# Hybrid attention and gMLP block in fp32: where tiles 3 and 4 of x are put, and when late weights and constants are loaded

## The chip, the cores and the metric

One core of a Trainium2 chip runs the whole block as one program. The metric is the time on the device in microseconds (us); lower is better. Three runs of the kernel before took 920.85, 924.07 and 924.38 us, so the median is 924.07 us. The profile comes from one further execution.

## The reference, cut to what matters

Everything is float32, with 1024 tokens and 1024 channels. One RMSNorm feeds one wide input projection. Two branches are computed from it, gated, summed, projected and added to x, and a last RMSNorm follows.

```python
h = rmsnorm(x, norm_g[l])
proj = h @ w_in[l]
q, k, v, za, u, vs, zs, gm = jnp.split(proj, IN_SPLITS, axis=-1)
...
a = window_sink_attention(q, k, v, att_sinks[l])
a = (a * jax.nn.silu(za)) @ w_att_out[l]
sgo = chunked_spatial_gating(jax.nn.gelu(u, approximate=False),
                             jax.nn.gelu(vs, approximate=False),
                             sg_w[l], sg_b[l], sg_ln_g[l], sg_ln_b[l])
sgo = (sgo * jax.nn.silu(zs)) @ w_sg_out[l]
ga, gs = jnp.split(jax.nn.sigmoid(gm + b_merge[l]), N_BRANCHES, axis=-1)
x = x + (ga * a + gs * sgo) @ w_o[l]
...
return rmsnorm(x, final_g)
```

The change lies in the first tenth of the program: the normalisation of x, the projection that makes `vs`, and the loads of what follows (the LayerNorm over `vs`, the mixing matrices and the projection that makes `u`).

## The kernel before, in words

**Products.** Each fp32 operand is split into a high and a low part in the type fp32r (`split`: ScalarE casts the high part, VectorE subtracts it to get the low one), and a product is three matmuls: high by high, high by low, low by high. On top of that every 1024-wide product is a two by two block scheme with seven block products instead of eight (Winograd's form of Strassen). For tokens the seven forms of the activations are called b11, t1, t2, b21, t3, b22, t4; each has a high and a low buffer of 128 x 4 x 512 (`T_b11h`, `T_t1l` and so on, one buffer each, made by `slot`). The weights' forms are a11, a12, s1, s2, s4, s3, a22.

**The first stage, `vs` (L703 to L862).** x comes in as eight tiles of 128 tokens. `scale_of(t)` loads a tile (unless it is in `x_in` already), squares it on ScalarE (L545) and makes the reciprocal root on VectorE; `turned_half` scales half of it in place on VectorE (L553) and transposes it on TensorE (L557) into a PSUM bank with the tag "sc", of which there are two. Tiles 0 to 3 (`first_tile`) give b11 and b21; tiles 4 to 7 (`second_tile`) give t1 and b22, and on the way a plain copy for t2, t3 and t4. Two DMAs with an add finish the latter for each of these tiles (`add_on`, L601 and L605, issued by GpSimd).

**Weights of `vs`.** a11 and a12 are loaded straight (into the places T_t3h and T_t3l). s1 is loaded into T_t4h in two halves, and then three pairs of adding DMAs run one behind the other, issued by GpSimd (L722 to L727): s1 += a22, a11 += s1 (this makes s2), a12 += a11 (this makes s4). s4 is split into `wh`, `wl` by `split_w("s4", c, behind=True)` (L746). s3 is loaded later into T_t4h again (L756) and added to (L758); a22 comes into two `wr` buffers (L764).

**Order of the matmuls.** `first_product(0..3)` (b11 by a11, b21 by a12), `by_s1(0)`, `by_s1(1)`, `by_s4(0)`, `by_s4(1)`, `by_s1(2)`, `by_s1(3)`, `by_s4(2)`, `by_s4(3)`, then three `late_product`s (t2 by s2, t3 by s3, t4 by a22). `by_s1` and `by_s4` are 12 matmuls of 128x512 for each tile. `gemm_pair` then makes `u`: its first call needs the first job's weights `r0` and `r1` and four sums of them (`make_sums`, L241 to L245, VectorE), which are split in turn by `split_next`.

**Queues.** Plain loads are all issued by SyncE (SP), adding DMAs by GpSimd (POOL); each engine issues in order, and a load waits at the head of its queue until its place is free. `raw_tile()` is a ring of three buffers with the tag "wr": x, a22 and the later weights go through it in turn. `after` orders two instructions of one engine; `behind` and `paced` make a DMA wait for a matmul, so that it is not sent too early. The order of the instructions on each engine is made by a scheduler from these constraints.

What follows is issued in this order by SP before the change: x0, a11, x1, a12, x2, the broadcast of norm_g (L716), s1, x3, x4, the first bias row (L889), x5, x6, x7, then behind the last transpose s3, a22 (L764), the mixing matrices (L789) and `r0`; behind the t2 product the five small constants (L831 to L841); then `r1`, whose `wr` buffer is the one of the first half of a22.

Of the kernel before, what the change touches and what calls it, by code (L numbers as in the profile page):

```python
# [24 lines left out]
F32 = mybir.dt.float32  # L25
# [5 lines left out]
P = 128  # L31
D = 1024
S = 1024
KC = D // P
# [18 lines left out]
def hybrid_tile(  # L53
# [16 lines left out]
    nc = tc.nc  # L70
# [15 lines left out]
    def mtile(shape, dt, tag, bufs, pool=None):  # L86
        return (pool or main).tile(shape, dt, name=nm(tag), tag=tag, bufs=bufs)
# [4 lines left out]
    def raw_tile():  # L92
        return mtile([P, D], F32, "wr", 3)
# [16 lines left out]
    sink_sb = const.tile([P, 8], F32, name="sink_sb")  # L110
    nsink_sb = const.tile([P, 8], F32, name="nsink_sb")
    bm_sb = const.tile([P, 16], F32, name="bm_sb")
    lg_sb = const.tile([P, KC], F32, name="lg_sb")
    lb_sb = const.tile([P, KC], F32, name="lb_sb")
# [43 lines left out]
    def after(second, first):  # L158

        tc.add_manual_dep(  # L160
            second.ins,
            first.ins.name,
            mybir.DependencyInfo(mybir.DependencyClass.NoSync, mybir.DependencyReason.DATA),
            reason="order",
        )
# [5 lines left out]
    def slot(name, shape=(P, 4, HALF), dt=F32R):  # L171

        return mtile(list(shape), dt, "T_" + name, 1)
# [28 lines left out]
    def begin_job():  # L202
        n = len(begun)
        if n < written[0]:
            begun.append(n)
            units.extend(jobs[n]())
# [25 lines left out]
    def half_of(half):  # L232
        return slice(half * HALF, (half + 1) * HALF)
# [46 lines left out]
    def paced(move):  # L280

        if pace[0] is not None:
            tc.add_manual_dep(
                move.ins,
                pace[0].ins.name,
                mybir.DependencyInfo(mybir.DependencyClass.Sync, mybir.DependencyReason.DATA),
                reason="pace",
            )
# [42 lines left out]
    term_of_x11 = [None]  # L331
# [149 lines left out]
    pool = outer.enter_context(tc.tile_pool(name="mixing", bufs=1))  # L481
# [4 lines left out]
    def load_x(t):  # L486
        xt = raw_tile()
        nc.sync.dma_start(xt[:], x[t * P : (t + 1) * P, :])
        return xt

    x_in = {0: load_x(0)}
# [18 lines left out]
    nf12 = [xtile() for _ in range(4)]  # L510
    f22 = []
# [4 lines left out]
    def x_place(i, j, t):  # L516
        return xh[:, 4 * j + t % 4, half_of(i)]
# [11 lines left out]
    casts, lows, turns = [], [], []  # L529

    def add_on(dst, src):
        return nc.gpsimd.dma_start(dst, src, accum_op=ALU.add)

    def behind(move, first):
        tc.add_manual_dep(
            move.ins,
            first.ins.name,
            mybir.DependencyInfo(mybir.DependencyClass.Sync, mybir.DependencyReason.DATA),
            reason="pace",
        )  # L540
# [48 lines left out]
    def second_tile(t):  # L589
        xt, r = scale_of(t)  # L590
        if t == 4:
            hb.update(new_b(("t1", "b22")))
            f22.append(slot("t4l", dt=F32))
        pt = turned_half(xt, r, 0)
        nc.vector.tensor_sub(raw_sum(t), raw_sum(t), pt[:])
        nc.scalar.mul(nf12[t - 4][:], pt[:], -1.0)
        form_of("t1", t, by_k(raw_sum(t)))
        pt = turned_half(xt, r, 1)
        form_of("b22", t, by_k(pt[:]))
        nc.scalar.copy(f22[0][:, t - 4, :], pt[:])  # L600
        add_on(nf12[t - 4][:], f22[0][:, t - 4, :])  # L601

    def raw_t2(t):
        nc.vector.tensor_add(raw_sum(t), raw_sum(t), f22[0][:, t - 4, :])
        return add_on(raw_b21(t), raw_sum(t))  # L605

    def w_vs(i, j, c):
        return w[W_VS + 4 * i + 2 * j + c]

    def two_k(v, c):  # L610
        return v[:, 2 * c : 2 * c + 2, :]

    def flat(v):
        return v.rearrange("p k n -> p (k n)")

    raws = {}

    def load_part(name, at, i, j, late=False):
        raws[name] = slot(at, dt=F32)
        for c in range(2):  # L620
            move = nc.sync.dma_start(flat(two_k(raws[name], c)), w_vs(i, j, c))
            if late:
                behind(move, turns[-1])

    def load_vs(c):
        nc.sync.dma_start(flat(two_k(raws["a11" if c < 2 else "a12"], c % 2)), w[W_VS + c])
# [34 lines left out]
    def vs_product(acc, name, t, weight, fresh, last=True, cs=(0, 1)):  # L661
        bh, bl = hb[name]
        for c in cs:
            for n in range(3):
                for k in (2 * c, 2 * c + 1):
                    wh, wl = vs_w[weight, k]
                    lt = (bh, bh, bl)[n][:, k, tokens(t)]
                    rt = (wh, wl, wh)[n]
                    mm = nc.tensor.matmul(
                        acc[:],  # L670
                        lt,
                        rt,
                        start=fresh and k == 0 and n == 0,
                        stop=k == 3 and n == 2,
                        skip_group_check=True,
                    )
        return mm

    accs = {}
    t5s = {}  # L680
# [10 lines left out]

    def by_s1(t):
        t5s[t] = bank("o" if t < 2 else "sc")
        vs_product(t5s[t], "t1", t, "s1", True)
        nc.scalar.mul(x_place(1, 1, t), t5s[t][:], -1.0)

    def by_s4(t):
        vs_product(t5s[t], "b22", t, "s4", False)
# [13 lines left out]
    for c in (2, 3):  # L712
        load_vs(c)
    x_in[2] = load_x(2)
    g_sb = xh[:, 6:8, HALF:D]
    nc.sync.dma_start(g_sb, norm_g.partition_broadcast(P).rearrange("p (h n) -> p h n", h=2))  # L716
    load_part("s1", "t4h", 1, 0)
    for c in (2, 3):
        split_vs(c)
    for move in unsplit:  # L720
# [23 lines left out]
    first_product(3)  # L744
    for c in range(2):
        split_w("s4", c, behind=True)  # L746
    second_tile(6)
    raw_t2(4)
    by_s1(0)
    by_s1(1)  # L750
    second_tile(7)
    for t in range(4):
        to_x11(t)
    for t in (5, 6, 7):
        last_of_h = raw_t2(t)
    load_part("s3", "t4h", 1, 0, True)  # L756
    for c in range(2):
        after(add_on(flat(two_k(raws["s3"], c)), w_vs(0, 0, c)), last_of_h)  # L758
    by_s4(0)
    by_s4(1)  # L760
    a22 = []
    for c in range(2):
        a22.append(raw_tile())
        behind(nc.sync.dma_start(a22[c][:], w_vs(1, 1, c)), turns[-1])  # L764
    by_s1(2)
    by_s1(3)
    split_w("s2", 0, behind=True)
# [13 lines left out]
    def gelu_of(t, half=0):  # L781
        two = xh[:, t : t + 2, half_of(half)]
        after(nc.scalar.activation(two, two, AF.Gelu), last_cast)
        if half == 0:
            for i in range(2):
                after(statistics(t + i, 0), lows[-1])

    mix_w = mtile([P, KC, P], F32, "wT", 1, pool)
    behind(nc.sync.dma_start(mix_w[:], sg_w), turns[-1])  # L789
    ones = mtile([P, P], F32R, "ones", 1, pool)  # L790
    nc.vector.tensor_scalar(ones[:], ident[:], 0.0, 1.0, op0=ALU.mult, op1=ALU.add)

    def late_product(name, weight, done, aside):
        for c in range(2):
            for t in range(4):
                pace[0] = vs_product(accs[t], name, t, weight, False, cs=(c,))
                if t % 2:
                    part_of_early(1)
                if c:
                    done(t)  # L800
                if aside:
                    aside.pop(0)()
# [25 lines left out]
        + [lambda: gelu_of(0), lambda: gelu_of(2)],  # L828
    )
    row_sums = [bank("sc") for half in range(2)]  # L830
    paced(nc.sync.dma_start(lg_sb[:], ln_g))  # L831
    paced(nc.sync.dma_start(lb_sb[:], ln_b))
    paced(nc.sync.dma_start(bm_sb[:], b_merge))
    of_head = sinks.rearrange("(c e r) -> e c r", e=2, r=2)
    for e in range(2):
        paced(
            nc.sync.dma_start(
                sink_sb[e * 64 : (e + 1) * 64].rearrange("p (c r) -> p c r", r=2),
                of_head[e].partition_broadcast(64),
            )  # L840
        )  # L841
    split_w("s3", 1)
    after(nc.vector.memset(mix_w[64:128, :, 0:64], 0.0), lows[-1])
    wh, wl = pair_of_w()
# [12 lines left out]
    split_w("a22", 1, a22[1][:])  # L857
    part_of_early(1)
    begin_job()
    late_product("t4", "a22", to_x21, [split_next, lambda: gelu_of(4, 1), lambda: gelu_of(6, 1)])  # L860
    for _ in range(2):
        split_next()  # L862
# [4 lines left out]
    late = []  # L867
# [17 lines left out]
    def bias_of(half):  # L885

        wT = mix_w[:, half * 4 : half * 4 + 4, :]
        bg = mtile([P, 4, P], F32, "bias", 1, pool)
        nc.sync.dma_start(bg[:].rearrange("p g i -> p (g i)"), sg_b[half_of(half)].partition_broadcast(P))  # L889
        for gg in range(4):  # L890
            g = half * 4 + gg
            nc.vector.scalar_tensor_tensor(
                bg[:, gg, :], row_sums[half][:, gg * P : (gg + 1) * P], lb_sb[:, g : g + 1], bg[:, gg, :], op0=ALU.mult, op1=ALU.add
            )
        return bg, wT

    bias = []
# [46 lines left out]
    pool = stage.enter_context(tc.tile_pool(name="keys", bufs=1))  # L944
# [44 lines left out]
    pool = stage.enter_context(tc.tile_pool(name="queries", bufs=1))  # L989
# [199 lines left out]
    pool = stage.enter_context(tc.tile_pool(name="attention", bufs=1))  # L1189
# [187 lines left out]
    pool = stage.enter_context(tc.tile_pool(name="later", bufs=1))  # L1377
# [508 lines left out]
```

## Time and profile before

| what | value |
|---|---|
| median of three runs | 924.07 us |
| profiled execution, its own time | 924.99 us |
| its span, first to last instruction | 923.2 us |
| mean granted clock of TensorE | 0.993 |
| TensorE busy with matmuls | 898.0 us |
| VectorE busy | 697.0 us |
| ScalarE busy | 527.3 us |
| GpSimd busy | 141.4 us |
| DMA moved | 209.57 MB, 227 GB/s in the mean |

A row of the timeline has the start in us, the busy time in us, the engine, the source line, the operation, the tile written and the tiles read, the shape, how many such instructions were merged, and in brackets how long the engine was idle before and what released it. A row of the windows has the busy time of each engine (and its number of instructions), the granted clock of TensorE, the DMA engines' busy share and the rate. A row of the chain of waits has start, duration and what the end of the program hung on in that time. "PE" is TensorE, "DVE" VectorE, "ACT" ScalarE, "POOL" GpSimd, "SPq" the queue of SyncE.

### The profile page before, as it was taken

The numbers are of one execution on the slowest core, as the hardware profiler recorded it, in microseconds if no ns is written. First come the engines' busy times: TensorE is split into PE (matmuls) and PEld (weight loads), VectorE is DVE, ScalarE is ACT, GpSimd is POOL, SyncE is SP. The second block draws the span as 40 slices with busy tenths as digits, with TensorE's granted clock in tenths as the row PEclk, the third lists the DMA queues.
The fourth block names the chain that finished last, engine by engine and source line by source line (L and its number), as shares of the span: only waits on it lengthen the run. The fifth ranks groups of instructions, "written<-read, shape, count | busy, mean of one in ns | idle before, by whom it ended". The sixth has DMA issues, their size and how long they took to land.

```text
span 923.2 us, 13181 instructions
## 1 busy us (share of the span) xinstructions
PE 898.0 (97%) x4284; PEld 746.0 (81%) x4284; DVE 697.0 (75%) x1263; ACT 527.3 (57%) x1058; POOL 141.4 (15%) x204
## 2 busy tenths in 40 slices
PE   8899899999999999999999999999998999999996
PEld 5678688888888778888888888888877887888885
DVE  6767786665678678887778888747797589579986
ACT  7666433334445366767766766755675475467443
POOL 1222112213011001111111111101100111210012
PEclk9999999999999999999999999999999999999999
DMA  8978878876788677778787788899869664998632
GB/s 292 220 179 213 248 237 179 175 151 200 245 282 259 228 222 182 186 184 200 196 207 235 251 245 188 225 318 369 307 212 324 243 197 153 308 299 287 205 114 115
DMA packets 131598, 209.57 MB, mean 227 GB/s; under 512 B 12649, under 2 KB 61033, under 8 KB 131530
## 3 DMA queue, kind: packets, MB, share of 16 engines
q1 hardware_dynamic: 110072, 149.74, 49.5%
q0 software_dynamic: 21312, 58.73, 27.9%
q8 instruction: 34, 0.56, 0.3%
q14 instruction: 34, 0.28, 0.1%
q10 hardware_dynamic: 146, 0.27, 0.1%
HBM read 147.74 MB, written 86.11 MB: 253 GB/s over the span
## 4 chain that ended last, share of the span: by engine, by line
PE 75%; DVE 10%; DMA 9%; issue 2%; ACT 1%; SPq 1%; POOL 0%; DVEq 0%; ACTq 0%; POOLq 0%
PE ps_mm L342 35%; PE ps_o L342 25%; PE ps_sc L1216 3%; DMA T_t4h<-in_w_dram 3%; PE ps_tp L342 3%; PE ps_o L1301 2%; PE ps_sc L342 2%; DMA wr<-in_w_dram 2%; PE ps_tp L1260 2%; DVE wl L156 2%; PE ps_tp L903 1%; DMA T_t3h<-T_t4h 1%; DVE bq L185 1%; DMA T_t3l<-T_t3h 1%; DVE bn L779 1%
## 5 line engine op out<-in xcount | busy, mean ns | idle before, releaser
L155 ACT CAST wh<-s 128x1024 fp32r<-128x1024 f32 (+1 forms) x78 | 78.2, 1005 | 95.6 <-PE ps_mm L342 49.4
L156 DVE TENSOR_TENSOR wl<-wr,wh 128x1024 fp32r<-128x1024 f32 (+1 forms) x78 | 73.1, 939 | 51.4 <-ACT wh L155 50.8
L155 ACT CAST wh<-wr 128x1024 fp32r<-128x1024 f32 (+1 forms) x78 | 64.0, 823 | 61.5 <-PE ps_mm L342 33.6
L156 DVE TENSOR_TENSOR wl<-s,wh 128x1024 fp32r<-128x1024 f32 (+1 forms) x78 | 91.0, 1166 | 10.5 <-ACT wh L155 10.3
L342 PE MATMUL ps_o<-T_t1h,wh 128*128 128x512 f32 x148 | 58.9, 398 | 0.7 <-ACT wh L155 0.7
L342 PE MATMUL ps_mm<-T_b11h,wh 128*128 128x512 f32 x140 | 55.8, 398 | 3.8 <-ACT xh L811 3.8
L342 PE MATMUL ps_mm<-T_b11h,wl 128*128 128x512 f32 x140 | 55.9, 399 | 2.9 <-DVE wl L156 2.9
L342 PE MATMUL ps_o<-T_b22h,wh 128*128 128x512 f32 x148 | 58.2, 393 | 0.0
L342 PE MATMUL ps_o<-T_b22l,wh 128*128 128x512 f32 x148 | 57.9, 391 | 0.0
L342 PE MATMUL ps_o<-T_b22h,wl 128*128 128x512 f32 x148 | 57.8, 390 | 0.0
L342 PE MATMUL ps_o<-T_t1h,wl 128*128 128x512 f32 x148 | 57.7, 390 | 0.0
L342 PE MATMUL ps_o<-T_t1l,wh 128*128 128x512 f32 x148 | 57.6, 389 | 0.0
L342 PE MATMUL ps_mm<-T_t4h,wh 128*128 128x512 f32 x140 | 55.6, 397 | 0.8 <-DVE x L377 0.8
L342 PE MATMUL ps_mm<-T_b11l,wh 128*128 128x512 f32 x140 | 55.8, 398 | 0.0
L342 PE MATMUL ps_mm<-T_t3l,wh 128*128 128x512 f32 x140 | 54.6, 390 | 0.6 <-DVE T_t3l L156 0.6
L342 PE MATMUL ps_mm<-T_t4h,wl 128*128 128x512 f32 x140 | 55.0, 393 | 0.0
L342 PE MATMUL ps_mm<-T_t3h,wh 128*128 128x512 f32 x140 | 54.9, 392 | 0.0
L342 PE MATMUL ps_mm<-T_t4l,wh 128*128 128x512 f32 x140 | 54.8, 391 | 0.0
L342 PE MATMUL ps_mm<-T_t3h,wl 128*128 128x512 f32 x140 | 54.7, 391 | 0.0
L1229 ACT ACTIVATE pr<-ps_sc,sm 128x192 f32<-128x192 f32 (+2 forms) x128 | 50.9, 410 | 6.6 <-DVE sm L1225 5.5
L342 PE MATMUL ps_mm<-T_t2l,wh 128*128 128x512 f32 x140 | 54.6, 390 | 0.0
L342 PE MATMUL ps_mm<-T_t2h,wl 128*128 128x512 f32 x140 | 54.6, 390 | 0.0
(384 smaller groups left out, 2399.8 us busy)
## 6 DMA issues: line engine op xcount, KB each, us to landing
wr<-in_w_dram SPq DMA_DIRECT2D x86, 256.0 KB
sums<-in_w_dram POOLq DMA_DIRECT2D x20, 512.0 KB, 9.3
s<-sums SPq DMA_DIRECT2D x20, 512.0 KB
q_hl<-qhl SPq DMA_DIRECT2D x16, 512.0 KB
q<-q_hl SPq DMA_DIRECT2D x64, 128.0 KB
y_dr<-x POOLq DMA_DIRECT2D x28, 256.0 KB, 6.5
wr<-in_w_dram SPq DMA_DIRECT2D x12, 512.0 KB
g<-in_w_dram POOLq DMA_DIRECT2D x12, 512.0 KB, 6.4
```

The source lines that it names most:

```text
L155: nc.scalar.copy(hi, src)
L156: return nc.vector.tensor_sub(lo, src, hi.bitcast(F32))
L185: op(dst[:, i : i + 2, :], a[:, i : i + 2, :], c[:, i : i + 2, :])
L342: nc.tensor.matmul(acc, lt, rt, start=fresh and k == 0 and n == 0, stop=k == 3 and n == 2, skip_group_check=True,)
L779: return nc.vector.bn_stats(stats[:, t, half, :], xh[:, t, half_of(half)])
L903: nc.tensor.matmul(pm[:, t * P : (t + 1) * P], xh[:, half * 4 + t, g * P : (g + 1) * P], bias[-1][1][:, g % 4, :], start=True, stop=True,)
L1216: nc.tensor.matmul(sc[:, i, k0:], q_of[:, c, i * P : (i + 1) * P], kt[:, f, k0:], start=f == 0, stop=f == 1,)
L1229: nc.scalar.activation(held_in[c, i], sc[:, i, lo:hi], AF.Exp, bias=nmax[:, c, i : i + 1], scale=-1.0, accum_out=sums[:, c, i : i + 1],)
L1260: nc.tensor.transpose(dst, pr[:, i, block * P : block * P + width], ident[:])
L1301: nc.tensor.matmul(po[:, cs], lt, rt, start=n == 0, stop=n == len(terms) - 1)
```

## The change

Tile t of x for t = 3 and 4 goes into T_t1l, the place of the low part of t1, which is not filled before tile 4 has been read. All of x is loaded from one place, and the first load of s1 stands ahead of the broadcast of norm_g. s3, a22, the small constants, the mixing matrices and the first bias row are issued behind the last matmul of `by_s1(0)` or `by_s1(1)`; the second half of a22 gets a buffer of the tag "s" instead of "wr", so that `r1` finds the third `wr` buffer free as soon as x7 has been read. The adds onto s3 stand ahead of those of tiles 6 and 7 in GpSimd's queue. The sums for `u` are tied to the last low part of t4.

```diff
@@ second_tile
-        add_on(nf12[t - 4][:], f22[0][:, t - 4, :])
+        return add_on(nf12[t - 4][:], f22[0][:, t - 4, :])
@@ load_part
-    def load_part(name, at, i, j, late=False):
+    def load_part(name, at, i, j, late=None):
         raws[name] = slot(at, dt=F32)
         for c in range(2):
             move = nc.sync.dma_start(flat(two_k(raws[name], c)), w_vs(i, j, c))
-            if late:
-                behind(move, turns[-1])
+            if late is not None:
+                behind(move, late)
@@ by_s1
-        vs_product(t5s[t], "t1", t, "s1", True)
+        mm = vs_product(t5s[t], "t1", t, "s1", True)
         nc.scalar.mul(x_place(1, 1, t), t5s[t][:], -1.0)
+        return mm
@@ loads of x and s1
     x_in[2] = load_x(2)
+    load_part("s1", "t4h", 1, 0)
     g_sb = xh[:, 6:8, HALF:D]
     nc.sync.dma_start(g_sb, norm_g.partition_broadcast(P).rearrange("p (h n) -> p h n", h=2))
-    load_part("s1", "t4h", 1, 0)
+    aside_x = slot("t1l", dt=F32)
+    for t in (3, 4):
+        x_in[t] = flat(two_k(aside_x, t - 3))
+        nc.sync.dma_start(x_in[t], x[t * P : (t + 1) * P, :])
+    for t in (5, 6, 7):
+        x_in[t] = load_x(t)
@@ after split_w("s4", c, behind=True)
-    second_tile(6)
+    mm = by_s1(0)
+    load_part("s3", "t4h", 1, 0, mm)
+    a22 = [raw_tile(), mtile([P, D], F32, "s", 2)]
+    for c in range(2):
+        behind(nc.sync.dma_start(a22[c][:], w_vs(1, 1, c)), mm)
+    behind(nc.sync.dma_start(lg_sb[:], ln_g), mm)
+    behind(nc.sync.dma_start(lb_sb[:], ln_b), mm)
+    behind(nc.sync.dma_start(bm_sb[:], b_merge), mm)
+    of_head = sinks.rearrange("(c e r) -> e c r", e=2, r=2)
+    for e in range(2):
+        behind(
+            nc.sync.dma_start(
+                sink_sb[e * 64 : (e + 1) * 64].rearrange("p (c r) -> p c r", r=2),
+                of_head[e].partition_broadcast(64),
+            ),
+            mm,
+        )
     raw_t2(4)
-    by_s1(0)
-    by_s1(1)
-    second_tile(7)
+    last_of_h = raw_t2(5)
+    for c in range(2):
+        move = add_on(flat(two_k(raws["s3"], c)), w_vs(0, 0, c))
+        after(move, last_of_h)
+    after(second_tile(6), move)
+    mm = by_s1(1)
+    after(second_tile(7), move)
+    mix_w = mtile([P, KC, P], F32, "wT", 1, pool)
+    behind(nc.sync.dma_start(mix_w[:], sg_w), mm)
+    first_bias = mtile([P, 4, P], F32, "bias", 1, pool)
+    behind(nc.sync.dma_start(first_bias[:].rearrange("p g i -> p (g i)"), sg_b[half_of(0)].partition_broadcast(P)), mm)
     for t in range(4):
         to_x11(t)
-    for t in (5, 6, 7):
-        last_of_h = raw_t2(t)
-    load_part("s3", "t4h", 1, 0, True)
-    for c in range(2):
-        after(add_on(flat(two_k(raws["s3"], c)), w_vs(0, 0, c)), last_of_h)
+    for t in (6, 7):
+        raw_t2(t)
     by_s4(0)
     by_s4(1)
-    a22 = []
-    for c in range(2):
-        a22.append(raw_tile())
-        behind(nc.sync.dma_start(a22[c][:], w_vs(1, 1, c)), turns[-1])
...
@@ ahead of the t4 product
+    term_of_x11[0] = lows[-1]
     late_product("t4", "a22", to_x21, [split_next, lambda: gelu_of(4, 1), lambda: gelu_of(6, 1)])
```

Left out are the lines that the moved loads had before (the mixing matrices, L788 and L789, the five small constants, L831 to L841) and the first bias row in `bias_of`, which is now `first_bias` for half 0. The scheduler's order on the engines differs too: on ScalarE the first of the two casts of s4 (L572, `wh<-T_t3l`) stood ahead of tile 5's last cast and copies and of the copy of `first_product(3)` (L687), and now stands behind them, next to the second; on TensorE the first four transposes of tile 6 now stand ahead of `by_s1(1)` instead of in its middle. The number of instructions on each computing engine is the same.

More of the change, by code (lines that the diff above doesn't have):

```diff
@@ L786, in gelu_of @@
                 after(statistics(t + i, 0), lows[-1])
-    mix_w = mtile([P, KC, P], F32, "wT", 1, pool)
-    behind(nc.sync.dma_start(mix_w[:], sg_w), turns[-1])
     ones = mtile([P, P], F32R, "ones", 1, pool)
@@ L830, in hybrid_tile @@
     row_sums = [bank("sc") for half in range(2)]
[L831 to L841, printed above, removed]
     split_w("s3", 1)
@@ L887, in bias_of @@
         wT = mix_w[:, half * 4 : half * 4 + 4, :]
-        bg = mtile([P, 4, P], F32, "bias", 1, pool)
-        nc.sync.dma_start(bg[:].rearrange("p g i -> p (g i)"), sg_b[half_of(half)].partition_broadcast(P))
+        bg = first_bias
+        if half:
+            bg = mtile([P, 4, P], F32, "bias", 1, pool)
+            nc.sync.dma_start(bg[:].rearrange("p g i -> p (g i)"), sg_b[half_of(half)].partition_broadcast(P))
         for gg in range(4):
```

## The prediction

> **What bounds the kernel now.** I read the page first, for which engine sets the time.
>
> ```profile
> span 923.2 us, 13181 instructions
> PE 898.0 (97%) x4284; PEld 746.0 (81%) x4284; DVE 697.0 (75%) x1263; ACT 527.3 (57%) x1058; POOL 141.4 (15%) x204
> ```
>
> TensorE works 898.0 of 923.2 us, so a gain has to come out of its gaps or its clock; the change removes no matmul. Next the waits of TensorE in the first 135 us, where every edit lies (us in total, times, longest).
>
> ```profile
> PE ps_mm L342 <- ACT xh L811: 3.8, 1, 3.8
> PE ps_o L669 <- ACT xh L687: 3.0, 1, 3.0
> ...
> PE ps_sc L557 <- ACT T_t4l L600: 1.1, 1, 1.1
> ```
>
> Three gaps, 7.9 of the 25 us. The chain of waits says what stands behind the two large ones.
>
> ```profile
> 5.89 10.73 DMA T_t4h<-in_w_dram
> ...
> 18.18 4.87 DMA T_t4h<-in_w_dram
> 23.04 11.10 DMA T_t3h<-T_t4h x2
> 34.14 8.59 DMA T_t3l<-T_t3h
> 42.80 1.04 ACT wh L572
> ...
> 90.44 12.43 DMA wr<-in_w_dram
> 102.97 0.69 DVE s L242
> ```
>
> The first is the row of adding DMAs that makes s4; its cast on ScalarE (42.80) has tile 5's casts queued behind it, and TensorE waits for those. The second is `r1`, which went out at 90.44, behind the split that frees its buffer.
>
> What a gap costs is seen in TensorE's timeline.
>
> ```profile
> 36.44 0.61 PE L669 MATMUL ps_o<-s,T_b21h 128*128 128x512 f32 x2
> 38.13 0.63 PE L557 MATMUL ps_sc<-ident,wr 128*128 128x128 f32 x4 [1.07 <-ACT T_t4l L600]
> 38.52 0.48 PE L669 MATMUL ps_o<-s,T_b21h 128*128 128x512 f32 x1
> ...
> 40.00 0.62 PE L669 MATMUL ps_o<-T_t2h,T_t1h 128*128 128x512 f32 x2
> ...
> 45.88 0.93 PE L669 MATMUL ps_o<-T_t2h,T_t1h 128*128 128x512 f32 x2 [2.97 <-ACT xh L687]
> ...
> 58.04 0.73 PE L669 MATMUL ps_sc<-T_t2h,T_t1h 128*128 128x512 f32 x2
> ...
> 69.06 0.62 PE L669 MATMUL ps_mm<-wh,T_t2h 128*128 128x512 f32 x2
> ...
> 102.18 0.61 PE L669 MATMUL ps_tp<-wh,T_t4l 128*128 128x512 f32 x2
> 106.57 0.50 PE L342 MATMUL ps_mm<-T_b11h,wh 128*128 128x512 f32 x1 [3.78 <-ACT xh L811]
> ...
> 110.93 0.48 PE L342 MATMUL ps_o<-T_t1h,wh 128*128 128x512 f32 x1
> ...
> 124.67 1.95 PE L903 MATMUL ps_tp<-wT,xh 128*128 128x128 f32 x16
> ```
>
> From 58.04 to 69.06 run 48 matmuls without a gap, 0.230 us each; that is the pace against which I measure.
>
> **First stretch, 36.44 to 58.04.** It holds 54 matmuls (12.4 us) and 24 transposes (four take 38.13 to 38.52, so 2.3 us): 14.7 us of work in 21.6, a loss of 6.9. Of it 4.0 are the two gaps; the rest is mostly slow pace behind them:
>
> ```profile
> 44.00:48.00 4.00, 2.12 (x6) 0.78 0.75 134
> ...
> 108.00:112.00 4.00, 4.00 (x13) 0.61 0.46 174
> ```
>
> The granted clock (third number) falls to 0.78 and 0.61 behind the two gaps, and comes back by itself. So 6.9 us is the most that this stretch can give. What is left of it after the change I work out along ScalarE and VectorE.
>
> ```profile
> 10.36 8.14 SPq L488 DMA_DIRECT2D wr<-in_x_dram  x2
> ...
> 32.70 1.06 ACT L545 ACTIVATE wT<-wr 128x1024 f32<-128x1024 f32 x1 [1.76 <-DMA wr<-in_x_dram]
> ...
> 42.80 1.04 ACT L572 CAST wh<-T_t3l 128x1024 fp32r<-128x1024 f32 x1 [2.71 <-DMA T_t3l<-T_t3h]
> ...
> 45.23 0.60 ACT L687 COPY xh<-ps_o 128x512 f32<-128x512 f32 x1
> ...
> 32.78 0.75 DVE L553 SCALAR_TENSOR_TENSOR wr<-wr,st,xh 128x512 f32<-128x512 f32 x1
> ...
> 37.28 1.41 DVE L553 SCALAR_TENSOR_TENSOR wr<-wr,st,xh 128x512 f32<-128x512 f32 x2
> ```
>
> *x5 earlier.* ScalarE's square of tile 5 waited 1.76 us for its load. In x0's buffer, free at 10.36, x3 went out; now x5 does, and behind the s1 halves, the broadcast, x3 and x4 (1.3 us each, below) it lands by some 22, so the square starts at 30.9. VectorE cannot take all of that: it is on tile 4 until 33.5, then come some 2.9 us of small steps and two low parts before tile 5's scaling. That starts at about 36.4 instead of 37.28, the transposes at 37.2 instead of 38.13, and `by_s1(0)` at 38.8 instead of 40.00.
>
> *The cast of s4 off tile 5's path.* On ScalarE tile 5's casts (0.6 us each) no longer stand behind it. They end at about 40.6, the copy of L687 at 41.2, and both s4 casts fit behind it, to 43.1. `by_s1(0)` is 12 matmuls, to 41.55; then VectorE, busy nearly throughout, is the one TensorE waits for. By the rows above (0.7 us a scaling or low part, 0.6 a copy on ScalarE, 1.05 and 1.2 a cast and low part of 1024 columns), tile 6's halves are scaled at 41.8 and 43.05 (waits of 0.3 and 0.2), tile 7's first at 50.1 (0.3), and `by_s1(2)` needs the bank of tile 7's transposes, which ScalarE leaves at 52.5 (0.3 more). Adding work and these, `by_s1(2)` starts at 52.5 instead of 58.04: **5.5 us**. None of these waits is as long as 1.07, and behind that one the matmul at 38.52 was still at full pace, so no slow clock is charged. As bounds: 6.9 from TensorE's work alone, 3.2 if the s4 chain still ends where it did (below).
>
> *Is s4 there by 41.2?* Its first link moves ahead of the broadcast. 0.5 MB cost this:
>
> ```profile
> 8.00:12.00 4.00, 3.66 (x13) 1.00 1.02 410
> ```
>
> 512 KB at 410 GB/s are 1.3 us, so s1's first half lands at 15.3 instead of 16.62. Of the links 4.87, 11.10 and 8.59, the last ran beside x7 and now has no x load beside it; nearest is 4.87 plus 1.3 for the other half's sharing, about 6. So 42.80 - 1.3 - 2.5 = 39. Ends of the range: 15.3 + 3 x 4.87 + issue = 31, and 42.8.
>
> [...]
>
> **58.04 to 102.6.** TensorE had no gap here, and everything on ScalarE and VectorE hangs on it and shifts along. s3 is issued at about 42 instead of this:
>
> ```profile
> 56.94 1.19 SPq L621 DMA_DIRECT2D T_t4h<-in_w_dram  x2
> ...
> 90.06 37.77 SPq L200 DMA_DIRECT2D wr<-in_w_dram  x10
> ```
>
> Earlier by more than the 5.5. The DMA engines have room for it: between 52 and 56 they stood at 0.08.
>
> ```profile
> 52.00:56.00 4.00, 4.00 (x21) 1.00 0.08 13
> ```
>
> The moved constants, matrices and bias cost nothing on TensorE, being wanted after 85; without that cover they would sit in SyncE's queue ahead of `r0` and `r1`, which are not wanted until 91. What is late next, if anything, are tile 6's and 7's adds, now behind s3's on GpSimd (rival D).
>
> **Second stretch, 102.6 to 124.67.** `r1`'s buffer is now x7's, free at about 51, so it lands some 30 us ahead of use.
>
> ```profile
> 94.72 2.34 DVE L156 TENSOR_TENSOR wl<-wr,wh 128x1024 fp32r<-128x1024 f32 x2
> 102.97 0.69 DVE L242 TENSOR_TENSOR s<-wr 128x512 f32<-128x512 f32 x1 [5.90 <-DMA wr<-in_w_dram]
> ...
> 104.97 1.04 ACT L155 CAST wh<-s 128x1024 fp32r<-128x1024 f32 x1 [9.80 <-DVE s L243]
> ...
> 102.97:123.36 20.39, 16.79 (x67) 13.69 (x68) 20.22 (x44) 10.69 (x15) 4.65 (x8) 0.92 0.73 221
> ```
>
> In the clock of before: VectorE makes the sums from 97.06, 5.9 us earlier; three adds of 0.6 later ScalarE casts them, 98.9 to 100, and then empties the four banks; the last groups of six matmuls end 1.4 us apart, the first at 98.5, so the first bank is free by 100.5. So the first product of `u` starts at 102.6 without a wait. Its 12 matmuls end at 105.35 at full pace; they ended at 110.93. Gain on TensorE: **5.6 us** (4.0 gap, 1.6 slow clock). The check is VectorE, busy 20.22 of 20.39 us from there to the last normalisation at 123.36, which the matmul at 124.67 needs: it starts 5.9 earlier and must wait for ScalarE's last gelu copy (103.3) only when it is level with it, so it ends at about 117.7, ahead of TensorE's 119.1. The bounds are 5.9 (VectorE's idle time) and 4.0 (the gap alone, if the pace is not regained).
>
> **Sum.** 5.5 + 5.6 = 11.1 us. The profiled execution took 924.99 us, so 913.9; it stands 0.9 above the median of the runs, so 913.0 is what I name.
>
> **The rivals.** A change under 0.5% (4.6 us) is not told from none by these measurements: faster is below 919.4, slower above 928.7.
>
> A, *VectorE sets the second stretch*. Its 20.2 us of work leave no slack; if its start follows ScalarE's banks (gap closed to 4.0) and small waits eat 1.5 more, the second gain is 2.5: 924.1 - 5.5 - 2.5 = 916. For it: 99% busy. Against: it starts 5.9 earlier. 0.15.
>
> B, *the adds starve behind the x loads*. Three loads of 1.3 us ahead of the first adds put the chain's end back to 42.8. Then the cast of s4 is on ScalarE to 43.8, the second to 46.3 instead of 43.1, and tiles 6 and 7 behind it are 2.3 us late, with the first gain at 3.2: 915.3. For it: adds beside loads took 11.10 against 4.87. Against: x4 to x7 were loaded inside this chain before, too. 0.12.
>
> C, *the change doesn't do what it says*: the wait of TensorE in the first stretch moves to VectorE's chain, and that gives only the 1.07. With 2.5 from the second stretch it is 924.1 - 3.6 = 920.5. For it: no row shows these small steps in their new order. Against: the 5.5 already leaves 1.1 us of such waits. 0.10.
>
> D, *slower: GpSimd's queue*. The adds of tile 6 wait in line until s3 has landed and both its adds are out. ScalarE's copy of `by_s4(2)` (L701) waits for tile 6's add and has the split of s2's second half queued behind it, which TensorE wants 24 matmuls behind 69.06, at 69 in the new time. The page's row for T_t4h:
>
> ```profile
> DMA to landing us min/median/max: 5.5/10.7/13.1
> ```
>
> At 13.1 for each of s3, its two adds (the second 4 later) and then tile 6's two, the copy would come at 42 + 13.1 + 13.1 + 4 + 7 = 79, the split 5 us later (copy, table load, gelu, cast, low part) at 84: a gap of 15 and 1.6 of slow clock, against the gain of 11.1: 929.6. It decides from a landing of tile 6's add at about 74. For it: in-order issue. Against: the idle DMA engines at 52; at 5.5 a link it lands near 60, when `by_s4(2)`, 36 matmuls behind `by_s1(2)`'s start, ends (60.8). 0.05.
>
> **How the numbers follow.** The forecast, 913.0, has 0.58, and its own bounds are 911.5 (6.9 + 5.9) to 915. A, B and C stand between it and no change. The range goes from 911 to 920, which leaves out D and a part of C. Faster: forecast, A and B, 0.85, less 0.04 for what they may be off, 0.81; same: 0.13; slower 0.06.
>
> **What would show it.** Right: no wait for L687 or the gelu copy (L811 before) above 0.5 us; `by_s1(2)` at 52.5; first product of `u` starting without a gap at about 97 and VectorE's sums without a DMA wait; clock 1.00 in both places. B: the cast of s4 still waits for its DMA past 41.2. A: the mixing matmuls wait for the normalisation. D: a DMA wait at the copy of `by_s4(2)`. Wrong altogether: a time above 919.4.

## Result and the profile after

| | before | after |
|---|---|---|
| median of the runs timed together | 921.1 us (5 runs) | 913.91 us (5 runs) |
| ratio, 95% interval | | 0.9913 (0.9886 to 0.9940) |
| profiled execution, its own time | 924.99 us | 915.36 us |
| span | 923.2 us | 913.6 us |

With two more executions timed beside the changed kernel, the median of before is 921.1 us, where three had given 924.07. The kernel became 7.2 us faster by the medians and 9.6 by the two profiled executions. The head of the page of after, with span and busy times:

```profile
span 913.6 us, 13183 instructions
PE 895.3 (98%) x4284; PEld 745.1 (82%) x4284; DVE 696.7 (76%) x1263; ACT 527.1 (58%) x1058; POOL 141.9 (16%) x204
```

TensorE does the same matmuls, and is busy 2.7 us less than before: the rest of the 9.6 us is gaps. Its waits in the first 135 us (in total, times, longest), some lines of that view; left out are one of 1.9 us (L498), which before has too, and 0.7 us in which it waited for nothing that the profile shows:

```profile
PE ps_sc L557 <- DVE wr L553: 0.4, 1, 0.4
PE ps_mm L669 <- ACT T_b11h L568: 0.3, 1, 0.3
PE ps_sc L669 <- ACT x L596: 0.2, 1, 0.2
```

The waits of 3.8, 3.0 and 1.1 us are gone. TensorE's timeline at the three places of the prediction:

```profile
53.03 0.73 PE L669 MATMUL ps_sc<-T_t2h,T_t1h 128*128 128x512 f32 x2 [0.24 <-ACT x L596]
...
97.62 0.39 PE L342 MATMUL ps_mm<-T_b11h,wh 128*128 128x512 f32 x1
...
113.95 1.95 PE L917 MATMUL ps_tp<-wT,xh 128*128 128x128 f32 x16
```

Against the profile of before, `by_s1(2)` starts 58.04 - 53.03 = 5.0 us earlier, and the first mixing matmul 124.67 - 113.95 = 10.7 us earlier. So by these two profiles the sum of the prediction came true. Which edit did it, and whether the first profile of before was typical, two profiles do not tell.

### The profile page after: what moved, and what is told of

Its sections match the earlier page's. It is cut to its first block, busy times and chain, and to the rows that moved or that the text cites. A ratio compares the mean times of both kernels' runs of the same rounds, so it can differ in the third digit from the quotient of the medians.

```text
span 913.6 us, 13183 instructions
## 1 busy us (share of the span) xinstructions
PE 895.3 (98%) x4284; PEld 745.1 (82%) x4284; DVE 696.7 (76%) x1263; ACT 527.1 (58%) x1058; POOL 141.9 (16%) x204
## 4 chain that ended last, share of the span: by engine, by line
PE 88%; DVE 7%; DMA 2%; issue 1%; ACT 1%; SPq 0%; DVEq 0%; ACTq 0%
PE ps_mm L342 37%; PE ps_o L342 27%; PE ps_sc L1230 3%; PE ps_mm L669 3%; PE ps_tp L342 3%; PE ps_tp L669 2%; PE ps_o L1315 2%; PE ps_sc L342 2%; PE ps_tp L1274 2%; PE ps_o L669 2%; PE ps_tp L917 2%; PE ps_sc L669 1%; DVE bq L185 1%; DVE wl L156 1%; DMA wr<-in_w_dram 1%
## 5 line engine op out<-in xcount | busy, mean ns | idle before, releaser
L156 DVE TENSOR_TENSOR wl<-wr,wh 128x512 fp32r<-128x512 f32 (+1 forms) x77 | 72.0, 936 | 51.3 <-ACT wh L155 50.7
L155 ACT CAST wh<-wr 128x512 fp32r<-128x512 f32 (+1 forms) x77 | 63.1, 821 | 62.6 <-PE ps_mm L342 34.2
L342 PE MATMUL ps_mm<-T_t2h,wh 128*128 128x512 f32 x140 | 55.0, 393 | 0.0
```

Source lines behind the costliest of these rows:

```text
L155: nc.scalar.copy(hi, src)
L156: return nc.vector.tensor_sub(lo, src, hi.bitcast(F32))
L342: nc.tensor.matmul(acc, lt, rt, start=fresh and k == 0 and n == 0, stop=k == 3 and n == 2, skip_group_check=True,)
```

## The experiments

Ratios are to the kernel before, run on the same chip, with 95% intervals.

**1. r1 early, alone** (`e1_r1_alone`; the kernel before with)

```diff
-    a22 = []
     for c in range(2):
-        a22.append(raw_tile())
+    a22 = [raw_tile(), mtile([P, D], F32, "s", 2)]
...
     begin_job()
+    term_of_x11[0] = lows[-1]
     late_product("t4", ...)
```

> The kernel before with one edit: the second half of a22 in a buffer of the tag s, so that r1 finds x7's buffer free (and the sums tied to the last low part of t4). Theory (the terms of the sum stand by themselves): TensorE's gap of 3.8 us at u's first product and the clock of 0.61 behind it go, the gaps of 3.0 (L687) and 1.1 (L600) stay, and the kernel is 5.6 us faster than before: a ratio of 0.994. Rival A of the prediction (VectorE sets the stretch): 2.5 us, 0.9973. Rival (r1 early collides with something that the rest of the change moves away): no gain, 1.000.

Measured: 914.3 us, 0.9929 (0.9901 to 0.9957). TensorE's waits in the first 135 us:

```profile
PE ps_sc L557 <- ACT T_t4l L600: 1.4, 1, 1.4
PE ps_o L669 <- ACT xh L687: 1.2, 1, 1.2
```

The gap of 3.8 is gone, as the theory had it. But the wait for L687 is 1.2 us and not 3.0, although nothing was edited that runs before it. That was the first sign that the first stretch varies from one execution to the next.

**2. The x loads and s1, alone** (`e2_x_alone`; the kernel before with)

```diff
+    load_part("s1", "t4h", 1, 0)
     g_sb = xh[:, 6:8, HALF:D]
     nc.sync.dma_start(g_sb, ...)
-    load_part("s1", "t4h", 1, 0)
+    aside_x = slot("t1l", dt=F32)
+    (x3, x4 into it, then load_x(5), load_x(6), load_x(7))
```

> The kernel before with one edit: tiles 3 and 4 of x into T_t1l, x5 to x7 loaded right behind, s1 ahead of the broadcast; nothing else. On ScalarE both casts of s4 then stand behind tile 5's casts and the copy of L687. Theory: this alone brings the first stretch, with the waits of 3.0 and 1.1 us gone and 5.0 us saved: a ratio of 0.9946; the gap of 3.8 at u's first product stays. Rival: without by_s1(0) placed ahead of tile 6 and the early s3 TensorE stops for tile 6's scaling, and only the 1.1 us of x5 are saved: 0.9988.

Measured: 920.27 us, 0.9988 (0.9971 to 1.0005), which cannot be told from no change: the rival's time, but not by the rival's way. The one long wait of TensorE that is left, and the chain of waits around it:

```profile
PE ps_mm L342 <- ACT xh L817: 7.1, 1, 7.1
```

```profile
75.03 6.41 DMA sink_sb<-in_sinks_dram
...
84.28 15.49 DMA wr<-in_w_dram
...
103.47 5.13 PE ps_mm L342 x12
```

The first stretch has no wait over 0.5 us, and the gap at `u`'s first product grew from 3.8 to 7.1: what was won before 60 us was waited away at 96. `r1` went out 6.2 us earlier than in before (84.28 against 90.44) and landed only 3.1 earlier, after 15.5 us under way. So the landing of `r1` does not follow its issue alone: the transfer itself is slow here.

**3. r1 late again** (`e3_no_r1`; the changed kernel with)

```diff
-    a22 = [raw_tile(), mtile([P, D], F32, "s", 2)]
+    a22 = [raw_tile(), raw_tile()]
```

> The changed kernel with one edit undone: both halves of a22 in wr buffers, so that r1 waits for the split of the first half again. Theory: the gap of 3.8 us at u's first product comes back with a clock near 0.6 behind it, and the time is 5.6 us above that of the changed kernel: a ratio to before of 0.9973 if the changed kernel stands at 0.9913. Rival: the earlier loads of everything else let r1 land in time, and the gap stays under 1 us: 0.9915 to 0.992.

Measured: 914.44 us, 0.9923 (0.9899 to 0.9948). The rival holds. SP's issues of `r1` (the first two of four) and VectorE's first sum:

```profile
84.73 6.70 SPq L200 DMA_DIRECT2D wr<-in_w_dram  x4
```

```profile
92.02 0.69 DVE L242 TENSOR_TENSOR s<-wr 128x512 f32<-128x512 f32 x1 [0.28 <-DMA wr<-in_w_dram]
```

`r1` goes out behind the split of a22 as in before, and is there 7.3 us after its first issue. The new buffer, on which the prediction built 5.6 us, is not needed when the rest of the change is there.

**4. x through the ring again** (`e4_no_x`; the changed kernel with)

```diff
-    aside_x = slot("t1l", dt=F32)
-    for t in (3, 4):
-        (x3, x4 into it)
-    for t in (5, 6, 7):
+    for t in (3, 4, 5, 6, 7):
         x_in[t] = load_x(t)
```

> The changed kernel with one edit undone: x3 and x4 go through the ring of wr buffers, so x5 waits for tile 2. Theory: tile 5's square waits for its load again, the gap of 1.1 us comes back, and with one cast of s4 ahead of tile 5's casts a gap of 2 to 3 us behind it: 4 to 5 us of the gain are lost, a ratio to before of 0.9957 to 0.9967. Rival: s1 ahead of the broadcast alone has the s4 chain early enough, and only 1.1 us are lost: 0.9925.

Measured: 913.83 us, 0.9919 (0.9896 to 0.9942): the rival is right that s1 ahead of the broadcast has the chain early enough. Its 0.9925 lies in the interval too, but the wait of 1.1 us that it names is not in the profile. TensorE's longest waits for another engine between 10 and 135 us:

```profile
PE ps_mm L669 <- ACT T_b11h L568: 0.3, 1, 0.3
PE ps_o L669 <- ACT xh L687: 0.2, 1, 0.2
```

Nor does tile 5's square wait for its load, which the edit was to bring back. In the six profiles with s1 behind the broadcast it waited 0.8 to 2.1 us; in experiment 8 below, whose only edit is s1 ahead of the broadcast, it does not wait, and `x` is in the ring there too. So the earlier s1 ends that wait by itself, and the new place of tiles 3 and 4 brings nothing that shows.

**5. The constants early, alone** (`e5_const_early`; the kernel before with)

```diff
     behind(nc.sync.dma_start(mix_w[:], sg_w), turns[-1])
+    behind(nc.sync.dma_start(lg_sb[:], ln_g), turns[-1])
+    (the other four likewise)
...
-    paced(nc.sync.dma_start(lg_sb[:], ln_g))
-    (the other four likewise)
```

> The kernel before with one edit: the five small constants issued behind the last transpose, right behind the mixing matrices, instead of behind the t2 product; r1 still waits for the split of a22's first half. Theory (the constants hold up the DMA engines, the sums issued by GpSimd pile up behind them, and r1 lands late in that pile): the DMA rate no longer falls to 47 GB/s in the 4 us ahead of r1's issue, r1 lands some 7 us after its issue instead of 12.4, the gap of 3.8 us at u's first product falls under 1, and the time is as with r1 early alone: a ratio of 0.993. Rival (r1's late issue is the cause, as the prediction had it): the gap stays at 3.8 and the ratio is 1.000.

Measured: 914.73 us, 0.9902 (0.9866 to 0.9939). The theory holds; by the intervals this edit alone cannot be told from the whole change. VectorE's first sum has no wait, with `r1` issued at 84.56:

```profile
91.48 0.68 DVE L242 TENSOR_TENSOR s<-wr 128x512 f32<-128x512 f32 x1
```

The windows show what the constants did. In the first profile of before, where SP issued them from 80.13 to 82.85 (the last numbers of a row are granted clock, DMA share and GB/s):

```profile
76.00:80.00 4.00, 4.00 (x20) 3.30 (x19) 4.00 (x8) 2.73 (x4) 0.69 (x1) 1.00 1.03 267
80.00:84.00 4.00, 4.00 (x19) 3.32 (x18) 4.00 (x7) 1.85 (x2) 1.38 (x2) 1.00 0.86 228
84.00:88.00 4.00, 4.00 (x19) 3.32 (x18) 3.62 (x6) 3.93 (x7) 0.69 (x1) 1.00 0.26 47
88.00:92.00 4.00, 4.00 (x20) 3.27 (x19) 4.00 (x7) 1.16 (x2) 1.41 (x3) 1.00 0.82 236
```

and in experiment 5, without them there:

```profile
84.00:88.00 4.00, 4.00 (x19) 3.31 (x18) 4.00 (x7) 2.24 (x3) 1.76 (x3) 1.00 0.76 208
```

GpSimd issues a sum of 512 KB (L296) every 2.72 us all through this time in before. From 80 to 84 the engines still move 228 GB/s. From 84 to 88, where 583 of 624 packets are under 512 bytes, they move 47 and are only 0.26 busy. The sums pile up: the one issued from 76 to 80 landed after 5.7 us, the one issued from 84 to 88 after 11.2, and `r1` shares the engines with the pile: from its issue to its landing, 90.4 to 102.9, the queue of the sums took 76.4% of the engines' time and SyncE's, with `r1`, 18.7%.

The third profile of before (experiment 12 below) is the nearest match: it starts `by_s1(2)` at 53.09, this one at 53.17, and it issues `r1` at 84.76. Its constants go out from 75.19 to 77.96. Its window behind them, the same window of this experiment, and its first sum:

```profile
80.00:84.00 4.00, 4.00 (x19) 3.34 (x18) 3.83 (x6) 3.13 (x5) 1.08 (x2) 1.00 0.29 75
```

```profile
80.00:84.00 4.00, 4.00 (x20) 3.30 (x19) 3.82 (x6) 2.93 (x4) 0.98 (x2) 1.00 0.82 239
```

```profile
96.45 0.69 DVE L242 TENSOR_TENSOR s<-wr 128x512 f32<-128x512 f32 x1 [4.68 <-DMA wr<-in_w_dram]
```

**6. s1 first and the constants early** (`e6_swap_and_const`; the kernel before with the edit of 5 and)

```diff
+    load_part("s1", "t4h", 1, 0)
     g_sb = xh[:, 6:8, HALF:D]
     nc.sync.dma_start(g_sb, ...)
-    load_part("s1", "t4h", 1, 0)
```

> The kernel before with two edits: s1 ahead of the broadcast of norm_g, and the constants behind the mixing matrices. x stays in the ring, s3 and a22 stay late, r1 waits for a22. Theory: these two carry the whole gain of the change: s4's first half lands near 36 to 38 us, the gaps of 3.0 and 3.8 us are gone, and the ratio is that of the changed kernel, 0.990 to 0.993. Rival: the first stretch needs by_s1(0) ahead of tile 6 or x in T_t1l as well; then only the second part shows, with a gap of over 1 us in the first stretch: about 0.995 to 0.997.

Measured: 913.78 us, 0.9893 (0.9863 to 0.9922), with no wait of TensorE over 0.5 us between 10 and 135 us. These two edits give the time of the whole change. How much of it the first of them adds to the second, 0.9902 and 0.9893 with their intervals do not tell.

**7. r1 and the constants late** (`e7_r1_and_const_late`; the changed kernel with the edit of 3, and the five constants `paced` behind the t2 product again)

> The changed kernel with two edits undone: both halves of a22 in wr buffers and the constants behind the t2 product; the rest of the change stays. Theory: either edit alone closes the gap at u's first product, without both it is back, and as long as with x alone (7.1 us, against 3.8 in before), so that most of the gain is lost: a ratio of 0.998. Rival (some other part of the change, such as the early s3 or mixing matrices, lets r1 land in time): the gap stays under 1 us: 0.992.

Measured: 919.85 us, 0.9974 (0.9950 to 0.9999): the time of the theory. The gap is back, though shorter in the profiled execution, which was the fastest of the ten runs (917.3 us):

```profile
PE ps_mm L342 <- ACT xh L821: 2.4, 1, 2.4
PE ps_tp L916 <- DVE x L932: 2.0, 1, 2.0
```

The second line is the prediction's rival A: with the sums late, TensorE's mixing waits for VectorE.

**8. s1 first, alone** (`e8_swap_alone`; the kernel before with the swap of 6)

> The kernel before with one edit: s1 ahead of the broadcast of norm_g. Theory: s4's first half lands 5 us earlier than in before (36 to 38 us), the gaps of the first stretch go, TensorE is some 5 us earlier at 60 us, and the gap at u's first product takes nearly all of it back (6 to 8 us in place of 3.8): a ratio of 0.998 to 1.000. Rival: the swap brings only the 1.3 us of the broadcast, the gaps of the first stretch stay at 1 us or more, and the ratio is 0.999 as well, but with a gap of 4 to 5 us at u's first product.

Measured: 920.14 us, 0.9965 (0.9944 to 0.9987), a little better than expected. s4's first half landed at 36.1 us, against 42.7 in the first profile of before. The gaps of the first stretch go, and the gap at `u`'s first product grows, as in 2, though to less than the 6 to 8 us of the theory:

```profile
PE ps_mm L342 <- ACT xh L811: 5.0, 1, 5.0
```

**9 and 12. The kernel before again** (`e9_before_again`, `e12_before_third`; unchanged)

> The kernel before, unchanged, profiled a second time. Theory (the sum was made against an execution at the slow end: the s4 chain's landing is a matter of chance, 42.7 us in the first profile, while two experiments whose program is the same up to there had it near 41 and 39.5): the gaps of the first stretch add up to 1 to 3.5 us instead of 4.1, the gap at u's first product is 3 to 7, longer where the first stretch was shorter, and the time is between 919 and 924. Rival (the gaps are fixed): 3.0, 1.1 and 3.8 again, within 0.2.

> The kernel before, unchanged, profiled a third time: as for the second, the first stretch's gaps between 1 and 4 us, the gap at u's first product between 3 and 7, and the sum of both nearer to constant than each (6 to 9 us).

Measured: 921.51 and 920.01 us, one run each. Start of `by_s1(2)`, `u`'s first product and the first mixing matmul, of the second profile:

```profile
53.95 0.72 PE L669 MATMUL ps_sc<-T_t2h,T_t1h 128*128 128x512 f32 x2
...
103.18 0.80 PE L342 MATMUL ps_mm<-T_b11h,wh 128*128 128x512 f32 x1 [4.47 <-ACT xh L811]
...
121.79 1.95 PE L903 MATMUL ps_tp<-wT,xh 128*128 128x128 f32 x16
```

and of the third:

```profile
53.09 0.72 PE L669 MATMUL ps_sc<-T_t2h,T_t1h 128*128 128x512 f32 x2
...
100.05 0.80 PE L342 MATMUL ps_mm<-T_b11h,wh 128*128 128x512 f32 x1 [2.20 <-ACT xh L811]
...
118.05 1.95 PE L903 MATMUL ps_tp<-wT,xh 128*128 128x128 f32 x16
```

The unchanged kernel reaches `by_s1(2)` at 53.95 and 53.09 in these, and at 58.04 in the profile on which the prediction stood. The second is as expected. The third is not: its gaps of the first stretch are 0.7 and 0.2 us and the other is 2.2, each below the range named, so the two gaps do not make up for each other to 6 to 9 us either. ScalarE's casts of s4 show the cause of the first (times of the first and the last start), in the first, second and third profile:

```profile
L572 ACT CAST wh<-T_t3l x2: 1044/1056/1067, 42.8 to 45.7; 128x1024 fp32r<-128x1024 f32 x2
```

```profile
L572 ACT CAST wh<-T_t3l x2: 1051/1059/1067, 40.3 to 43.2; 128x1024 fp32r<-128x1024 f32 x2
```

```profile
L572 ACT CAST wh<-T_t3l x2: 1048/1050/1053, 39.4 to 42.4; 128x1024 fp32r<-128x1024 f32 x2
```

In the first and second the cast waits for its DMA (2.7 and 1.4 us), in the third it doesn't: the same chain of adds ended at 42.7, 40.2 and 38.6 us.

**10. The changed kernel again** (`e10_after_again`; unchanged)

> The changed kernel, unchanged, profiled again. Theory: its early gaps are no matter of chance (s4 lands 3 to 4 us ahead of its use, r1 20 us), so no wait over 0.5 us in the first 135 us, and the time is 912 to 915.5; with the runs of before pooled the ratio is 0.989 to 0.993. The clock behind the unchanged wait of 1.6 us near 314 us may or may not fall to 0.6 to 0.8; if it doesn't, the time is near 913 and the gain stays at about 11 us against the first profile of before.

Measured: 913.54 us, 0.9893 (0.9857 to 0.9928), with no wait over 0.5 us between 10 and 135 us. The places of the three profiles above:

```profile
52.83 0.73 PE L669 MATMUL ps_sc<-T_t2h,T_t1h 128*128 128x512 f32 x2 [0.24 <-ACT x L596]
...
113.74 1.95 PE L917 MATMUL ps_tp<-wT,xh 128*128 128x128 f32 x16
```

Both are within 0.21 us of the first profile of after: in these two, what is early hardly varies. The clock near 316 fell again, to 0.61 (last section), in an execution of 913.22 us.

**11. The sums later** (`e11_sums_later`; the kernel before with)

```diff
     def late_product(...):
...
-                if t % 2:
-                    part_of_early(1)
...
     def both():
-        part_of_early(1)
+        for _ in range(2 if hooks[0] < 26 else 1):
+            part_of_early(1)
```

(and without the one sum behind the split of a22's second half)

> The kernel before with one edit: none of the thirteen sums that GpSimd issues between the t2 product and u's first product; they go out later, two at a time. r1 still waits for the split of a22's first half and the constants still go out behind the t2 product. Theory (r1 lands late in the pile of sums that the constants held up): with no sums there r1 lands 3 to 5 us behind its issue, and the gap at u's first product is under 1 us. Rival (the constants' packets themselves hold up r1): it still lands 12 us behind its issue, and the gap is 3 us or more. The time is left open, as the sums now run beside the loads of u's weights.

Measured: 921.75 us (one run). The constants go out from 75.14, `r1` at 84.69. Windows, SP's issues and VectorE's first sum:

```profile
76.00:80.00 4.00, 4.00 (x20) 3.30 (x19) 3.80 (x7) 2.09 (x3) 0.00 (x0) 1.00 0.08 5
80.00:84.00 4.00, 4.00 (x19) 3.32 (x18) 3.82 (x6) 3.06 (x5) 0.00 (x0) 1.00 0.05 5
```

```profile
84.69 6.70 SPq L200 DMA_DIRECT2D wr<-in_w_dram  x4
```

```profile
91.62 0.68 DVE L242 TENSOR_TENSOR s<-wr 128x512 f32<-128x512 f32 x1
```

```profile
GB/s 0 0 0 0 0 0 0 0 92 143 297 420 369 440 379 369 82 31 0 0 0 0 0 0 0 0 0 0 0 0 0 0 41 0 0 0 0 61 174 266
```

The last row is the rate in 40 slices of 0.2 us from 84 to 92 us: all of `r1` moves between 85.6 and 87.6, within 3 us of its issue, with its buffer as late as in before and the constants as late as in before. The third profile of before issues both at these times to 0.1 us, and its first sum had to wait until 96.45. So the constants do not hold up `r1` themselves; the pile of sums does. The time is no better than before: TensorE was 11.3 us ahead of the first profile of before at 120 us, but 5.0 ahead at 142. The chain of waits names a store of 256 KB beside the sums, which now go out two at a time; TensorE waited 3.3 us behind it:

```profile
119.60 15.23 DMA s_dr<-x
...
134.93 0.59 ACT x L367
...
135.57 5.49 PE ps_mm L342 x12
```

## Why the prediction was right, and where it was not

In short: in before, `r1` goes out late and then lands late in a pile of sums that five small loads have held up, and TensorE waits. The change sends `r1` early and moves the small loads away; each of the two is enough. The prediction saw the first of these and not the second.

*The time.* 913.0 was named with 911 to 920, and 913.91 came out. This is right for the changed kernel, whose early part ran without gaps in both its profiles, as the sum assumed. The gain by medians is smaller than the 11.1 of the sum: 7.2, or 922.3 - 913.9 = 8.4 with the 58 runs of before timed for comparison and all 11 of after taken together. So that the time came out within 0.9 us is partly luck: the start, 924.07, stood 1.8 above the 922.3 of all runs, and the gain was named 2.7 too large. The bounds stated with it do not follow from their terms either: 6.9 and 5.9 give 911.3, and 3.2 and 4.0 give 916.9 where 915 is named. That the gain lies in the early part the profiles do show: the first mixing matmul started at 124.67, 121.79 and 118.05 us in the three of before, at 113.95 and 113.74 in the two of after, 7.9 us apart in the middle, and what follows took 797.7 to 800.2 us in all five.

*First stretch, 5.5 us: the mis-sized term.* Against the profile used it measured 5.0. But the six executions with no edit that acts before it started `by_s1(2)` at 58.04, 54.77 (experiment 1), 53.17 (5), 53.95 (9), 53.04 (11) and 53.09 (12), with 53.6 in the middle; the changed kernel at 53.03 and 52.83. In the middle the term is about 0.6 us. The prediction took its gaps (3.0 and 1.1) from the one of the six in which this stretch was slowest, and corrected only 0.9 us, for the whole program. The step that failed is "The profiled execution took 924.99 us, so 913.9; it stands 0.9 above the median": it stands 2.7 above the median of all 58, and a surplus in the whole does not say how large the surplus in one chain of DMAs is.

*What the first stretch rests on.* The forecast had *x5 earlier* and *the cast of s4 off tile 5's path*. Experiment 4 does without the first and loses nothing, as the earlier s1 ends tile 5's wait too (experiment 8). That the earlier s1 link brings the chain forward was judged rightly: with s1 ahead of the broadcast the cast of s4 never waited in any profile (after and experiments 2, 3, 4, 6, 7, 8, 10), while without it the cast waited in the first profile of before and in experiments 1, 9 and 11 (0.5 to 2.7 us). That steadiness shows more clearly than the 0.6 us.

*Rival B.* The adds do run slower behind the early x loads (s4's first half landed at 36.9 to 37.8 us in the five profiles that have them, at 36.1 to 36.2 in experiments 4, 6 and 8, where s1 is early and x is not), but within the slack: that rival's condition, a cast of s4 still waiting for its DMA past 41.2, never came. No run shows three loads of 1.3 us ahead of the first adds, which its 42.8 counts on; the landings show 0.7 to 1.7 us between the two groups.

*Second stretch, 5.6 us: right in size, with half of the cause.* From `by_s1(2)` to the first mixing matmul before took 124.67 - 58.04 = 66.6, 67.8 and 65.0 us in its three profiles, after 60.9 in both: 4.0 to 6.9 gained, 5.7 in the middle. But the step "`r1`'s buffer is now x7's ... so it lands some 30 us ahead of use" is only one of two ways to it. The other is in the step "The moved constants, matrices and bias cost nothing on TensorE", which asked what the move costs and not what it frees. By experiments 1, 3, 5 and 7 either edit closes the gap and without both it is back: the two do not add.

*From one gap to the next.* The forecast took the two stretches as independent. In before they are not: much of what the first wins, the second waits away, as `r1` lands when the pile of sums lets it. Experiment 2 started `by_s1(2)` at 51.67 and `u`'s first product only at 103.47; the third profile of before started them at 53.09 and 100.05. Experiments 2 and 8, each with a first stretch free of waits over 0.5 us, gained 1.1 us, not clear of none, and 3.2 (0.0012 and 0.0035 of 921 to 922). Hence most of the gain hangs on the second stretch.

*Rivals A, C and D.* A's wait was over 0.5 us in experiment 7 alone. C fell: no TensorE wait of the first stretch moved to VectorE beyond 0.4 us. D's queue is to be seen in ScalarE's timeline of after, but only at tile 7 and off TensorE's path:

```profile
67.84 0.59 ACT L702 COPY xh<-ps_sc 128x512 f32<-128x512 f32 x1 [1.61 <-DMA xh<-xh]
```

Of the named signs, the gap-free first product came at 97.62, the clock of 1.00 at both places, and VectorE's sums without a DMA wait; `by_s1(2)` came at 53.03 for 52.5.

*Left open.* How the constants' packets stop the sums is not shown, only that the rate falls behind their issue and not where they are absent. Why the adds of s4 end between 38.6 and 42.7 us in the same program was not tried.

## What to carry to other kernels

Before building on a gap in a profile that ends in a chain of DMAs, profile the same kernel two or three times: here one gap was 3.0 us in the first execution and 1.6 and 0.2 in the next two, and the other was there each time. When a load lands late, look at who else is on the DMA engines between its issue and its landing before moving its issue. And test each edit alone and each left out: here two of a dozen edits, moving one load and five small ones, gave the time of the whole change, and the one that its title names first gave nothing that shows.

## What the runs showed of the hardware

In these runs small loads cost another queue far more than their bytes. In experiment 11, alone, the constants moved at 5 GB/s and kept the engines 0.08 and 0.05 busy in the two windows from 76 to 84 us. Beside the sums, in the first profile of before, the rate fell from 267 by way of 228 to 47 GB/s in the three windows from 76 to 88 us. SyncE's queue moved 0.03, 0.01 and 0.01 MB in them and took 2.0, 4.9 and 7.4% of the engines' time; the queue of the sums moved 1.04, 0.90 and 0.16 MB, in the last 15% of the first.

TensorE's clock fell behind short gaps in some executions (to 0.64 and 0.61 in the two of after) and not in others (1.00 in the first two of before). A wait that the change doesn't touch, of the profile of before and of after:

```profile
326.79 1.39 PE L1216 MATMUL ps_sc<-k,q 128*128 128x128 f32 x8 [1.62 <-ACT pr L1229]
```

```profile
315.72 1.39 PE L1230 MATMUL ps_sc<-k,q 128*128 128x128 f32 x8 [1.49 <-ACT pr L1243]
```

The windows that hold the matmuls behind it, in after and in experiment 10:

```profile
316.00:320.00 4.00, 3.99 (x16) 3.17 (x16) 2.33 (x13) 3.02 (x16) 0.00 (x0) 0.64 0.75 187
```

```profile
316.00:320.00 4.00, 4.00 (x16) 3.15 (x16) 2.40 (x14) 3.26 (x15) 0.00 (x0) 0.61 0.77 182
```

and in the first profile of before:

```profile
328.00:332.00 4.00, 4.00 (x22) 3.31 (x22) 2.95 (x13) 3.98 (x18) 0.00 (x0) 1.00 0.87 195
```

It takes some 1.6 us of an execution that has it: the lead of the first profile of after on the first of before is 326.79 - 315.72 = 11.07 us at these matmuls and 330.28 - 320.77 = 9.51 at the next product of `ps_o`. For experiment 10 an estimate from its window, 4 us at 0.61, is 4 x 0.39 = 1.6 as well. The unchanged kernel has it too: at the same place the clock stayed at 1.00 behind 1.79 us in its second profile and fell to 0.72 behind 1.80 in its third. Nor does the length of a wait decide at `u`'s first product: the matmuls behind 2.36 us in experiment 7 started 0.23 us apart, the full pace, and the clock fell to 0.59 behind 2.20 in the third profile of before. It fell behind 1.49 us and not behind 1.62 or 1.79; what decides it is not shown.
